# A two-layer decoder trunk in fp32: conditioning summed beside the heads' projections, branch sums on VectorE, value matmuls of 512 columns

## The chip, the core and the metric

The kernel runs on one core of a Trainium2 chip. The metric is the device time of one execution in microseconds (us). A core has TensorE (PE) for matmuls, VectorE (DVE), ScalarE (ACT) and GpSimd (POOL) for elementwise work, and SyncE (SP), on whose queue this kernel issues its DMAs. Each engine runs its instructions in the order in which the program lists them, and semaphores make it wait for the others.

## The reference, cut to what matters

Two layers over a sequence of 512 with 1024 channels, all in float32. Each layer conditions its input with scales and shifts that are computed from a vector `c`, runs three branches (retention, a gated linear recurrence called HGRN2, a causal convolution of 31 taps with its own layer norm), merges them with sigmoid gates, projects, and normalizes; then a feed-forward part with a norm of its own.

```python
cond = jax.nn.silu(c)
for l in range(DEPTH):
    mod = cond @ w_ada[l] + b_ada[l]
    sh1, sc1, g1, sh2, sc2, g2 = [m[:, None, :] for m in jnp.split(mod, 6, axis=-1)]
    h = x * (1.0 + sc1) + sh1
    y = _token_mixer(h, ...)
    x = _layer_norm(ALPHA * x + g1 * y, ln1_g[l], ln1_b[l])
    h = x * (1.0 + sc2) + sh2
    y = _conv_ffn(h, ...)
    x = _layer_norm(ALPHA * x + g2 * y, ln2_g[l], ln2_b[l])

# in _token_mixer: p = h @ w_in, split into rq, rk, rv, rg, gq, gf, gi, gg, ca, cb, gates
u = _causal_dwconv(ca * jax.nn.sigmoid(cb), conv_w, conv_b)      # 31 taps, 512 channels
u_c = jax.nn.silu(_layer_norm(u, conv_ln_g, conv_ln_b))
gates = jax.nn.sigmoid(gates.reshape(bsz, s, N_BRANCH, D_MODEL))
y = gates[:, :, 0] * (u_a @ w_branch[0])
y = y + gates[:, :, 1] * (u_b @ w_branch[1])
y = y + gates[:, :, 2] * (u_c @ w_branch[2])
return y @ w_out
```

## The kernel before, in words

Channels lie on the 128 partitions, the 512 positions along the free axis. Each float32 product is made of three matmuls (`mm3`, L249 to L251): every operand is kept as a high part and a low part, and high·high, high·low and low·high are added up in one PSUM tile. Weights come in chunks of 512 KB (128 x 1024 float32). `prefetch` issues the DMA (L215, tile `wr`), copies the high part on ScalarE (L216, `wh`) and subtracts the low part on VectorE (L217, `wl`); `chunk` keeps two chunks ahead of the matmuls. A projection of 128 channels is 24 matmuls of 512 columns on one chunk (`proj`, tile `pm`).

The conditioning `cond @ w_ada` does not run on PE: each of its 96 columns is a chunk of 512 KB that is loaded (L191, tile `ar`) and multiplied and summed on VectorE (L195, then L196). Its tile has the tag `raw`, with four buffers, and these are the buffers of the weight chunks too.

A layer goes through these stages: the projections for the convolution; ten steps of heads (`MIX`: for HGRN2 and for retention, a projection of the values for all four heads by `proj_tok`, and three projections for each head, with the head's own small matmuls run beside the next head's projections); the three branches in the order HGRN2, retention, convolution (`ORDER = (1, 0, 2)`, by index 1, 0, 2), where each step makes two gate projections and two branch products (L249 to L251 with a `b` tile as input), multiplies them (L782) and adds them to the sum (L786 on GpSimd, tile `ys`); the output projection with the first norm; and the feed-forward part.

Work that PE does not need soon runs as generators. `tick`, called within each projection, adds to a credit; while the credit is positive the generators in `heads` and in the list `fill` are stepped, and what each step yields is taken off. `fill` holds, in this order, the tables for the rotation, the convolution's taps (`conv_taps`, two times two tiles, L383), its norm (`conv_norm`: totals on GpSimd L396 to L398, `exact2` L236 and L237, a column sum on PE L243 and L245, subtraction L408, square L410, totals and column sum again, `rstd` L308 to L311, product L421, SiLU L422, `split` L229 and L231), and the remaining conditioning (`rest`). Before the third branch's first product a loop sees to it that the norm is issued:

```python
while b == 2 and len(u_c) < 4:
    step(fill, fill[0])
```

The generators fix what is issued, and with which priority; a scheduler then sets each engine's order, from its own estimate of when each instruction can run.

Of the kernel before, what the change touches and what calls it, by code (L numbers as in the profile page):

```python
# [20 lines left out]
P = 128  # L21
KT = D // P
# [6 lines left out]
EPS = 1e-5  # L29
NB = 47  # L30
NHL = 4
LA = 2
NRAW = 4
TK = 1.7
AUX = 99
TG = 1.1
# [17 lines left out]
def w_plan(l):  # L54
    conv = [SEG[s] + 128 * i for i in range(4) for s in ("cb", "ca")]
    if l == 0:
        plan = [("octo", k, conv) for k in range(8)]
    else:
        plan = [("quad", k, conv[:4]) for k in range(4)]
        plan += [("in", c) for c in conv[4:]]  # L60

    def tok(seg):
        return [("tok", c, SEG[seg] + 256 * g) for g in range(2) for c in range(2)]

    for what, i in MIX:
        if i < 0:
            plan += tok("gi" if what == "g" else "rv")
        else:
            names = ("gf", "gq", "gg") if what == "g" else ("rq", "rk", "rg")
            plan += [("in", SEG[n] + 128 * i) for n in names]  # L70
    for b in ORDER:
        for jp in range(4):
            c = SEG["gates"] + D * b + 256 * jp
            plan += [("in", c), ("in", c + 128), ("br", b, jp)]
    plan += [("out", j) for j in range(8)]
    plan += [("upq", k, [0, DFF, 128, DFF + 128]) for k in range(4)]
    for j in range(2, FT):
        plan += [("up", j), ("up", FT + j)]
    plan += [("down", c) for c in range(FT)]
    return plan  # L80
# [9 lines left out]
def trunk(ctx, tc, xT, cT, pos, ada, bada, wts, cols, lbl, rope_c, decay, hmask, outT):  # L90
# [97 lines left out]

    def ada_col(l, i):
        raw = wp.tile([P, 1024], F32, tag="raw", name=nm("ar"), bufs=NRAW)  # L190
        nc.sync.dma_start(raw, ada[l, i])  # L191
        o = ADA[i]
        dst = modt[l][:, o:o + 1]
        yield 0.0
        stt(raw, raw, 1.0, cond, ALU.mult, ALU.mult, accum_out=dst)  # L195
        ts(dst, dst, bad[:, 48 * l + o:48 * l + o + 1], 1.0 if o // 8 in (1, 4) else 0.0, ALU.add, ALU.add)  # L196
        yield 1.3

# [91 lines left out]
    def proj_tok(hs):  # L290
        for g in range(2):
            w = [chunk("tok", LA - 1), chunk("tok", LA - 1)]
            for tp in range(2):
                q = pm()
                for t2 in range(2):
                    tk = 2 * tp + t2
                    dst = q[:, 256 * t2:256 * (t2 + 1)]
                    for kt in range(KT):
                        mm3(dst, sl2(hs[kt], 128 * tk), sl2(w[kt // 4], 256 * (kt % 4), 256),
                            kt == 0, kt == KT - 1)  # L300
                    tick(1.5)
                yield g, tp, q

# [70 lines left out]

    def conv_taps(l, i0, us, out, aux):

# [4 lines left out]
        for d in range(1, CK):  # L381
            for i, a in enumerate(acc):
                stt(a[:, d:S], us[i][:, 0:S - d], col(l, "cw", 4 * (CK - 1 - d) + i0 + i), a[:, d:S],  # L383
                    ALU.mult, ALU.add)
            yield 1.2
            if d % AUX == 0 and aux:
                yield from aux.pop(0)

    def rest(aux):
        while aux:  # L390
            yield from aux.pop(0)

# [252 lines left out]
    def affine(l, gname, bname, lm, sc, sh):  # L645
        for j in range(8):
            G, B = gbt[:, j:j + 1], gbt[:, 8 + j:9 + j]
            tt(G, col(l, gname, j), mod(lm, sc, j), ALU.mult)
            stt(B, col(l, bname, j), mod(lm, sc, j), mod(lm, sh, j), ALU.mult, ALU.add)
        o = CO[gname]  # L650
        ts(gbt[:, 16:24], colt[l][:, o:o + 8], ALPHA, None, ALU.mult)
        o = CO[bname]
        ts(gbt[:, 24:32], colt[l][:, o:o + 8], ALPHA, None, ALU.mult)

    def norm_to_h(nrm, hs, a, b):
# [37 lines left out]
    for j in range(8):  # L693
        cs = [ada_col(0, 2 * j), ada_col(0, 2 * j + 1)]
        for g in cs:
            next(g)
        nc.sync.dma_start(X[j], xT[j])
        for g in cs:
            next(g)
        prefetch()  # L700
# [7 lines left out]
    for l in range(L):  # L708
# [4 lines left out]
        CS = [big(), big()]  # L713
        aux = [ada_col(l, i) for i in range(16, 40)]
        if l == 0:
            tables()
        fill.append(rope_tables(CS))
        for i in (0, 2):
            us = []
            for t in range(2):  # L720
                if not qs:
                    qs = [proj(chunk("in"), hs), proj(chunk("in"), hs)]
                us.append(conv_gate(qs.pop(0), qs.pop(0)))
            fill.append(conv_taps(l, i, us, acc, aux))
        fill.append(conv_norm(l, acc, u_c))
        fill.append(rest(aux))

        vg, vr = [big() for _ in range(4)], [big() for _ in range(4)]
        for what, h in MIX:
            if what == "g" and h < 0:  # L730
                for g, tp, q in proj_tok(hs):
                    for t2 in range(2):
                        act(vg[2 * tp + t2][:, 256 * g:256 * (g + 1)], q[:, 256 * t2:256 * (t2 + 1)], AF.Copy)
            elif h < 0:
                for g, tp, q in proj_tok(hs):
                    qv = q.rearrange("p (t h d) -> p t h d", h=2, d=128)
                    sm = bp.tile([P, 4], F32, tag="sm", name=nm("sm"), bufs=2)
                    nc.vector.tensor_reduce(sm, q.rearrange("p (a d) -> p a d", d=128),
                                            mybir.AxisListType.X, ALU.add)
                    for t2 in range(2):  # L740
                        stt(vr[2 * tp + t2][:, 256 * g:256 * (g + 1)].rearrange("p (h d) -> p h d", d=128),
                            sm[:, 2 * t2:2 * t2 + 2].unsqueeze(2).broadcast_to([P, 2, 128]), -1.0 / 128,
                            qv[:, t2], ALU.mult, ALU.add)
            elif what == "g":
                qf = proj(chunk("in"), hs)
                qq = proj(chunk("in"), hs)
                qg = proj(chunk("in"), hs)
                drain(heads, 2)
                heads.append(hgrn_head(l, h, *hgrn_gates(l, h, qq, qf, qg), vg, u_b))
            else:  # L750
                q = rope(proj(chunk("in"), hs), *CS)
                k = rope(proj(chunk("in"), hs), *CS)
                qg = proj(chunk("in"), hs)
                sg = big()
                act(sg, qg, AF.Silu)
                drain(heads, 2)
                heads.append(ret_head(l, h, q, k, sg, vr, u_a))

        ys = [None] * 8
        for bi, b in enumerate(ORDER):  # L760
            us = (u_a, u_b, u_c)[b]
            for jp in range(4):
# [13 lines left out]
                for t in range(2):  # L776
# [14 lines left out]
        affine(l, "ln1g", "ln1b", l, 4, 3)  # L791
        nrm = Norm(l, 2)
# [26 lines left out]

        fill.extend(ada_col(l, i) for i in range(40, 48))  # L820
        gs = []
# [19 lines left out]
        if l == 0:  # L841
            fill.extend(ada_col(1, i) for i in range(16))
        nrm = Norm(l, 5)
        hs = []
        held = []
        for j in range(8):
            parts = HALVES if j == 7 else ((0, S),)
            if l == 0 and j == 7:
                drain(fill)
                affine(l, "ln2g", "ln2b", 1, 1, 0)  # L850
            for a, b in parts:
# [38 lines left out]
def _chunks(l, w_in, w_branch, w_out, w_up, w_down):  # L890
    out = np.empty((NW, 128, 1024), np.float32)
    down = w_down.reshape(FT, 128, 8, 128).transpose(2, 0, 1, 3).reshape(FT, 8, 128, 128)
    for i, p in enumerate(W_PLAN[l]):
# [10 lines left out]
        elif p[0] == "tok":  # L904
            out[i] = _ktile(w_in, 4 * p[1], 4, p[2], 256)
        elif p[0] == "br":
# [77 lines left out]
```

## Time and profile before

| | us |
|---|---|
| median of 3 runs | 1848.71 (1846.3 to 1849.69) |
| the profiled execution | 1850.63 |
| its span (first to last instruction) | 1848.5 |
| PE busy | 1805.8 (98%) |
| VectorE busy | 1292.6 (70%) |
| ScalarE busy | 748.4 (40%) |
| GpSimd busy | 225.8 (12%) |
| weight chunks | 299 DMAs of 512 KB, median 3.5 from issue to landing |
| conditioning chunks | 96 DMAs of 512 KB, median 4.3 |

An instruction's duration reaches from its start to its end. On PE matmuls overlap, so the durations of neighbours add up to more than the time they take; the distance between starts is what one of them costs. The same holds, by a smaller part, on VectorE. In the rows below, "idle before" in brackets is the time in which the engine waited before the instruction, with what ended it. PEclk is the granted TensorE clock as a share of 2.4 GHz.

### The profile page before, as it was taken

The page shows a single profiled execution, that of the slowest core. Times are in us where ns is not written, and L with a number is a line of the kernel's source. Part 1 is how long each engine was busy: PE and PEld are TensorE (multiplying, and loading weights), DVE is VectorE, ACT ScalarE, POOL GpSimd, SP SyncE. Part 2 cuts the span into 40 slices and gives each one's busy share as a digit, 9 for nine tenths or more (in the row PEclk, how much of TensorE's full clock was granted, in tenths as well). Part 3 has the DMA queues.
Part 4 walks back from the last instruction along what each step waited for, and adds up shares of the span by engine and source line. Part 5 has one row for each costly group of instructions (what it writes and reads, how often), then busy time and mean ns, then how long its engine had stood idle before and what let it go on. Part 6 is the DMA issues. An engine that isn't in the chain of part 4 may idle for free.

```text
span 1848.5 us, 23499 instructions
## 1 busy us (share of the span) xinstructions
PE 1805.8 (98%) x9156; PEld 1520.1 (82%) x9156; DVE 1292.6 (70%) x2026; ACT 748.4 (40%) x1034; POOL 225.8 (12%) x193
## 2 busy tenths in 40 slices
PE   7999999999999999999999999999999999999997
PEld 5888877888788888888889987778788988888886
DVE  6995565977869756667499565993775896666354
ACT  2434344333337444422263344453523464444222
POOL 3111231042100000000000221320322000000002
PEclk9999999999989999999999999999999999999998
DMA  8512222226614422255222121222474243222221
GB/s 301 197 69 80 75 75 80 91 104 212 230 70 142 144 102 92 102 182 184 93 87 103 69 75 69 80 74 99 161 241 148 92 146 128 103 92 102 92 80 46
DMA packets 63614, 217.81 MB, mean 118 GB/s; under 512 B 7440, under 2 KB 9872, under 8 KB 63504
## 3 DMA queue, kind: packets, MB, share of 16 engines
q1 hardware_dynamic: 63504, 216.32, 34.0%
q8 instruction: 72, 1.18, 0.3%
q14 instruction: 38, 0.31, 0.0%
HBM read 214.19 MB, written 2.10 MB: 117 GB/s over the span
## 4 chain that ended last, share of the span: by engine, by line
PE 81%; DVE 10%; DMA 3%; issue 2%; POOL 2%; ACT 2%; POOLq 0%; SPq 0%; DVEq 0%; ACTq 0%
PE pm L249 24%; PE pm L251 24%; PE pm L250 24%; DMA ar<-ada 3%; DVE wl L217 2%; PE ps L477 2%; POOL b L786 1%; DVE ar L195 1%; DVE b L383 1%; DVE x L642 1%; PE po L552 1%; PE ps L544 1%; DVE b L782 1%; PE ps L250 1%; PE ps L251 0%
## 5 line engine op out<-in xcount | busy, mean ns | idle before, releaser
L249 PE MATMUL pm<-h,wh 128*128 128x512 f32 (+1 forms) x1568 | 612.7, 391 | 13.7 <-ACT wh L216 12.1
L251 PE MATMUL pm<-h,wl 128*128 128x512 f32 (+1 forms) x1568 | 602.6, 384 | 0.1
L250 PE MATMUL pm<-h,wh 128*128 128x512 f32 (+1 forms) x1568 | 601.6, 384 | 0.0
L217 DVE TENSOR_TENSOR wl<-wr,wh 128x1024 fp32r<-128x1024 f32 (+1 forms) x301 | 376.4, 1253 | 250.5 <-ACT wh L216 249.4
L216 ACT ACTIVATE wh<-wr 128x1024 fp32r<-128x1024 f32 (+1 forms) x301 | 317.1, 1055 | 489.3 <-PE pm L250 387.2
L249 PEld LDWEIGHTS pm<-h,wh 128*128 128x128 f32 x1568 | 295.5, 188 | 72.9 <-ACT wh L216 12.1
L251 PEld LDWEIGHTS pm<-h,wl 128*128 128x128 f32 x1568 | 295.0, 188 | 61.1 <-DVE wl L217 3.1
L250 PEld LDWEIGHTS pm<-h,wh 128*128 128x128 f32 x1568 | 295.4, 188 | 58.7 <-issue 1.9
L249 PE MATMUL pm<-b,wh 128*128 128x512 f32 (+1 forms) x764 | 280.6, 367 | 5.6 <-ACT b L229 4.2
L250 PE MATMUL pm<-b,wh 128*128 128x512 f32 (+1 forms) x764 | 279.6, 366 | 0.3 <-DVE b L231 0.2
L251 PE MATMUL pm<-b,wl 128*128 128x512 f32 (+1 forms) x764 | 279.0, 365 | 0.0
L383 DVE SCALAR_TENSOR_TENSOR b<-b,cols,b 128x511 f32<-128x511 f32 (+14 forms) x240 | 171.6, 769 | 0.0
L249 PEld LDWEIGHTS pm<-b,wh 128*128 128x128 f32 x764 | 144.8, 190 | 30.3 <-ACT b L229 5.4
L250 PEld LDWEIGHTS pm<-b,wh 128*128 128x128 f32 x764 | 144.9, 190 | 24.5 <-DVE b L231 1.5
L251 PEld LDWEIGHTS pm<-b,wl 128*128 128x128 f32 x764 | 145.0, 190 | 22.8
L195 DVE SCALAR_TENSOR_TENSOR ar<-ar,cond 128x1024 f32<-128x1024 f32 x96 | 123.8, 1296 | 57.1 <-DMA ar<-ada 56.9
L229 ACT ACTIVATE b<-b 128x512 fp32r<-128x512 f32 x88 | 55.5, 630 | 232.8 <-DVE b L832 109.2
L231 DVE TENSOR_TENSOR b<-b,b 128x512 fp32r<-128x512 f32 x88 | 61.1, 694 | 53.8 <-ACT b L229 53.6
L490 POOL TENSOR_TENSOR b<-b,b 128x256 f32<-128x256 f32 x64 | 56.4, 881 | 324.1 <-PE ps L477 217.3
L786 POOL TENSOR_TENSOR b<-b,b 128x512 f32<-128x512 f32 x32 | 57.2, 1786 | 234.9 <-DVE b L782 222.5
L249 PE MATMUL pm<-wh,h 128*128 128x256 f32 x256 | 73.6, 288 | 0.0
L250 PE MATMUL pm<-wl,h 128*128 128x256 f32 x256 | 72.3, 283 | 0.6 <-DVE wl L217 0.6
(205 smaller groups left out, 1904.1 us busy)
## 6 DMA issues: line engine op xcount, KB each, us to landing
wr<-wts SPq DMA_DIRECT2D x299, 512.0 KB, 3.5
ar<-ada SPq DMA_DIRECT2D x96, 512.0 KB, 4.3
x<-xT SPq DMA_DIRECT2D x8, 256.0 KB, 5.9
b<-decay SPq DMA_DIRECT2D x8, 256.0 KB, 3.7
outT<-b SPq DMA_DIRECT2D x16, 128.0 KB, 1.8
b<-hmask SPq DMA_DIRECT2D x3, 256.0 KB, 5.9
cond<-cT SPq DMA_DIRECT2D x1, 512.0 KB, 4.5
wr<-wts SPq DMA_DIRECT2D x2, 256.0 KB, 7.3
```

Source lines behind the costliest of these rows:

```text
L195: stt(raw, raw, 1.0, cond, ALU.mult, ALU.mult, accum_out=dst)
L216: act(hi[:, s], raw[:, s], AF.Copy)
L217: tt(lo[:, s], raw[:, s], hi.bitcast(F32)[:, s], ALU.subtract)
L229: act(hi, src, AF.Copy)
L231: tt(lo, src, hi.bitcast(F32), ALU.subtract)
L249: mm(dst, a[0], b[0], start=first, stop=False)
L250: mm(dst, a[0], b[1], start=False, stop=False)
L251: last[0] = mm(dst, a[1], b[0], start=False, stop=end)
L383: stt(a[:, d:S], us[i][:, 0:S - d], col(l, "cw", 4 * (CK - 1 - d) + i0 + i), a[:, d:S], ALU.mult, ALU.add)
L477: mm(z[:, 64 * i:64 * (i + 1)], ke[:, sl], rhs, start=True, stop=True)
L490: ptt(kv[:, :, 0, :], kv[:, :, 0, :], fv[:, :, 1:2].broadcast_to([P, nb, m]), ALU.mult)
L786: ptt(ys[j], ys[j], sg[t], ALU.add)
```

## The change

Four parts. Conditioning chunks get buffers of their own (tag `ada`, three of them), and a generator `ada_cols` issues the next load before it sums a column. The 24 columns of a layer's first norm are stepped once per head projection (`proj_cond`), and what a step yields (1.4) is taken off the credit; columns that are left are appended to `fill`, and the affine terms of the norm follow as a generator. The branch sums move from GpSimd (`ptt`) to VectorE (`tt`). `proj_tok` multiplies with 512 columns of weights at a time, so its chunks are cut as two channel tiles by 512 columns, four are held, and a result tile covers one block of 128 positions and all four heads; the evictions follow suit. `conv_taps` no longer carries conditioning. There is one `B` buffer more, and the program is built with `dynamic_dma_scratch_size=1024`.

```diff
+NADA = 3
-AUX = 99
...
     def tok(seg):
-        return [("tok", c, SEG[seg] + 256 * g) for g in range(2) for c in range(2)]
+        return [("tok", c, SEG[seg]) for c in range(4)]
...
-    def ada_col(l, i):
-        raw = wp.tile([P, 1024], F32, tag="raw", name=nm("ar"), bufs=NRAW)
+    def ada_load(l, i):
+        raw = wp.tile([P, 1024], F32, tag="ada", name=nm("ar"), bufs=NADA)
         nc.sync.dma_start(raw, ada[l, i])
+        return raw
+
+    def ada_sum(l, i, raw):
         o = ADA[i]
         dst = modt[l][:, o:o + 1]
-        yield 0.0
         stt(raw, raw, 1.0, cond, ALU.mult, ALU.mult, accum_out=dst)
         ts(dst, dst, bad[:, 48 * l + o:48 * l + o + 1], 1.0 if o // 8 in (1, 4) else 0.0, ALU.add, ALU.add)
-        yield 1.3
+
+    def ada_cols(l, idx):
+
+        raw = None
+        for i, j in zip(idx, [*idx[1:], None]):
+            if raw is None:
+                raw = ada_load(l, i)
+                yield 0.2
+            nxt = None if j is None else ada_load(l, j)
+            ada_sum(l, i, raw)
+            raw = nxt
+            yield 1.4
...
     def proj_tok(hs):
-        for g in range(2):
-            w = [chunk("tok", LA - 1), chunk("tok", LA - 1)]
-            for tp in range(2):
-                q = pm()
+
+
+        w = []
+        for tp in range(2):
+            qs = [pm(), pm()]
+            for c in range(4):
+                if tp == 0:
+                    w.append(chunk("tok", LA if c < 2 else 3 - c))
                 for t2 in range(2):
-                    tk = 2 * tp + t2
-                    dst = q[:, 256 * t2:256 * (t2 + 1)]
-                    for kt in range(KT):
-                        mm3(dst, sl2(hs[kt], 128 * tk), sl2(w[kt // 4], 256 * (kt % 4), 256),
+                    for k in range(2):
+                        kt = 2 * c + k
+                        mm3(qs[t2], sl2(hs[kt], 128 * (2 * tp + t2)), sl2(w[c], 512 * k, 512),
                             kt == 0, kt == KT - 1)
-                    tick(1.5)
-                yield g, tp, q
+                    if t2:
+                        tick(1.5)
+            for t2 in range(2):
+                yield 2 * tp + t2, qs[t2]
...
-        aux = [ada_col(l, i) for i in range(16, 40)]
+        aux = ada_cols(l, range(16, 40))
...
-            fill.append(conv_taps(l, i, us, acc, aux))
+            fill.append(conv_taps(l, i, us, acc))
         fill.append(conv_norm(l, acc, u_c))
-        fill.append(rest(aux))
+
+        def proj_cond(hs):
+
+            credit[0] -= next(aux, 0.0)
+            return proj(chunk("in"), hs)
...
-                qf = proj(chunk("in"), hs)
-                qq = proj(chunk("in"), hs)
-                qg = proj(chunk("in"), hs)
+                qf, qq, qg = [proj_cond(hs) for _ in range(3)]
...
+        fill.append(aux)
+        fill.append(affine(l, "ln1g", "ln1b", l, 4, 3))
...
-                        ptt(ys[j], ys[j], sg[t], ALU.add)
+                        tt(ys[j], ys[j], sg[t], ALU.add)
...
-        fill.extend(ada_col(l, i) for i in range(40, 48))
+        fill.append(ada_cols(l, range(40, 48)))
...
-            fill.extend(ada_col(1, i) for i in range(16))
+            fill.append(ada_cols(1, range(16)))
```

In the changed file the line numbers are higher: the sum of a column is L197 and L198, a weight's parts are L228 to L230, `mm3` is L262 to L264, the column sum L256 and L258, the taps L401, the norm's subtraction L420, `rstd` L326 to L329, the branch's product L795 and its sum L799.

The first place is PE in layer 0, around the second column sum of the convolution's norm. `pm_3371` and `pm_3389` are the branch products of a step of the second branch, `po_3384` is the column sum; the first column sum (`po_3294`) stands 50 rows above it, and the first matmul on the convolution's result 132 rows below it. Before:

```order
L250 MATMUL pm_3371<-b_2746,wh_3276 128x512
L251 MATMUL pm_3371<-b_2744,wl_3277 128x512
L243 MATMUL po_3384<-b_3347,avg_r 128x512
L245 MATMUL po_3384<-b_3348,avg_r 128x512
L249 MATMUL pm_3389<-b_2072,wh_3276 128x512
L250 MATMUL pm_3389<-b_2074,wh_3276 128x512
```

Now `pm_3387` is the second gate projection of the third branch, `po_3439` and `po_3463` are the two column sums, and `pm_3502` is the first product on the convolution's result (`b_3474`, `b_3476`):

```order
L262 MATMUL pm_3387<-h_265,wh_3307 128x512
L263 MATMUL pm_3387<-h_266,wh_3307 128x512
L264 MATMUL pm_3387<-h_265,wl_3308 128x512
L256 MATMUL po_3439<-b_3435,avg_r 128x512
L258 MATMUL po_3439<-b_3436,avg_r 128x512
L256 MATMUL po_3463<-b_3459,avg_r 128x512
L258 MATMUL po_3463<-b_3460,avg_r 128x512
L262 MATMUL pm_3502<-b_3474,wh_3347 128x512
L263 MATMUL pm_3502<-b_3476,wh_3347 128x512
```

The matmuls between the two column sums, and those between the second one and its reader, have gone from there; in layer 1 the same rows are neighbours too.

The second place is VectorE in layer 0 at the last taps. Before, they end in the second branch (`b_2783` and `b_2784` are the last pair's sums, `pm_3236` a product of the second branch):

```order
L782 TENSOR_TENSOR b_3112<-pm_3137,b_3112 128x512
L217 TENSOR_TENSOR wl_3193<-wr_3191,wh_3192 128x1024
L383 SCALAR_TENSOR_TENSOR b_2784<-b_508,cols_272,b_2784 128x483
L383 SCALAR_TENSOR_TENSOR b_2783<-b_505,cols_272,b_2783 128x482
L383 SCALAR_TENSOR_TENSOR b_2784<-b_508,cols_272,b_2784 128x482
L217 TENSOR_TENSOR wl_3232<-wr_3230,wh_3231 128x1024
L217 TENSOR_TENSOR wl_3277<-wr_3275,wh_3276 128x1024
L782 TENSOR_TENSOR b_3189<-pm_3236,b_3189 128x512
```

Now the product on `pm_3329`, the last matmuls of the second branch, stands before the last 18 taps (`b_3046` and `b_3047`), of which the first four are shown; the others follow without anything between, down to 128x482:

```order
L230 TENSOR_TENSOR wl_3348<-wr_3346,wh_3347 128x1024
L795 TENSOR_TENSOR b_3304<-pm_3329,b_3304 128x512
L401 SCALAR_TENSOR_TENSOR b_3046<-b_505,cols_272,b_3046 128x490
L799 TENSOR_TENSOR b_2832<-b_2832,b_3304 128x512
L401 SCALAR_TENSOR_TENSOR b_3047<-b_508,cols_272,b_3047 128x490
L230 TENSOR_TENSOR wl_3383<-wr_3381,wh_3382 128x1024
L401 SCALAR_TENSOR_TENSOR b_3046<-b_505,cols_272,b_3046 128x489
L401 SCALAR_TENSOR_TENSOR b_3047<-b_508,cols_272,b_3047 128x489
```

The taps' end has moved from the second branch to after its end. In layer 1 the last tap stands just before VectorE's product on the last matmuls of the second branch.

The third place is SP's queue in layer 0's heads. Before, the loads of weights stand there alone:

```order
L215 DMA wr_1266<-wts 128x1024
L215 DMA wr_1272<-wts 128x1024
L215 DMA wr_1456<-wts 128x1024
L215 DMA wr_1462<-wts 128x1024
L215 DMA wr_1506<-wts 128x1024
```

Now conditioning loads (`ar`) stand between them, up to eight in a row:

```order
L228 DMA wr_1324<-wts 128x1024
L191 DMA ar_1807<-ada 128x1024
L191 DMA ar_1886<-ada 128x1024
L191 DMA ar_1957<-ada 128x1024
L191 DMA ar_2012<-ada 128x1024
L191 DMA ar_2083<-ada 128x1024
L191 DMA ar_2146<-ada 128x1024
L191 DMA ar_2219<-ada 128x1024
L191 DMA ar_2282<-ada 128x1024
L228 DMA wr_1378<-wts 128x1024
```

All of the later columns' loads have moved into layer 0, those of the feed-forward part and of layer 1 too; before, the first of them after the start stands in the third branch.

## Rows read from the trace of the kernel before

**Rows 1.** The page: span, PE's busy time, the chain that ended last.

```profile
span 1848.5 us, 23499 instructions
...
PE 1805.8 (98%) x9156; PEld 1520.1 (82%) x9156; DVE 1292.6 (70%) x2026; ACT 748.4 (40%) x1034; POOL 225.8 (12%) x193
...
PE 81%; DVE 10%; DMA 3%; issue 2%; POOL 2%; ACT 2%; POOLq 0%; SPq 0%; DVEq 0%; ACTq 0%
```

**Rows 2.** Timeline of PE, 480 to 520: start, duration, operation, idle before.

```profile
499.43 0.39 PE L251 MATMUL pm<-b,wl 128*128 128x512 f32 x1
...
511.70 0.80 PE L249 MATMUL pm<-b,wh 128*128 128x512 f32 x1 [2.29 <-ACT b L229]
...
518.09 0.40 PE L251 MATMUL pm<-b,wl 128*128 128x512 f32 x1
```

**Rows 3.** Windows: length, busy of PE, PEld, DVE, ACT, POOL; PEclk, DMA share, GB/s.

```profile
60.00:400.00 340.00, 338.57 (x1855) 286.35 (x1856) 252.38 (x381) 137.76 (x195) 62.05 (x58) 1.00 0.25 86
512.00:518.00 6.00, 6.00 (x14) 4.41 (x14) 2.26 (x3) 1.06 (x1) 0.00 (x0) 0.50 0.30 100
1110.00:1250.00 140.00, 135.79 (x653) 106.16 (x653) 120.36 (x175) 64.53 (x92) 35.06 (x28) 1.00 0.21 72
```

**Rows 4.** The chain of waits, 400 to 520: start, length, what.

```profile
486.81 4.63 DMA ar<-ada
...
497.89 3.33 DMA wr<-wts
```

**Rows 5.** The page's groups: busy and mean ns of one, idle before.

```profile
L249 PE MATMUL pm<-h,wh 128*128 128x512 f32 (+1 forms) x1568 | 612.7, 391 | 13.7 <-ACT wh L216 12.1
...
L195 DVE SCALAR_TENSOR_TENSOR ar<-ar,cond 128x1024 f32<-128x1024 f32 x96 | 123.8, 1296 | 57.1 <-DMA ar<-ada 56.9
...
L249 PE MATMUL pm<-wh,h 128*128 128x256 f32 x256 | 73.6, 288 | 0.0
```

**Rows 6.** Timeline of PE, value projection of layer 0, 64 to 70.

```profile
63.89 0.28 PE L249 MATMUL pm<-wh,h 128*128 128x256 f32 x1
...
69.89 0.28 PE L250 MATMUL pm<-wl,h 128*128 128x256 f32 x1
```

**Rows 7.** Timeline of PE, projections, 340 to 345.

```profile
339.97 0.39 PE L249 MATMUL pm<-h,wh 128*128 128x512 f32 x1
...
344.95 0.39 PE L250 MATMUL pm<-h,wh 128*128 128x512 f32 x1
```

**Rows 8.** Timeline of VectorE: weight part, taps, the norm's subtraction.

```profile
339.28 1.23 DVE L217 TENSOR_TENSOR wl<-wr,wh 128x1024 fp32r<-128x1024 f32 x1
340.42 4.03 DVE L383 SCALAR_TENSOR_TENSOR b<-b,cols,b 128x507 f32<-128x507 f32 x6
...
403.19 2.48 DVE L408 SCALAR_TENSOR_TENSOR b<-po,b 128x512 f32<-128x512 f32 x4
```

**Rows 9.** Timeline of GpSimd, the norm's totals and low part, layer 0.

```profile
391.06 2.21 POOL L397 TENSOR_TENSOR b<-b,b 128x512 f32<-128x512 f32 x1 [1.23 <-DVE b L383]
393.34 1.29 POOL L398 TENSOR_TENSOR b<-b,b 128x512 f32<-128x512 f32 x1
396.49 1.33 POOL L237 TENSOR_TENSOR b<-b,b 128x512 fp32r<-128x512 f32 x1 [1.85 <-ACT b L236]
...
407.91 2.37 POOL L397 TENSOR_TENSOR b<-b,b 128x512 f32<-128x512 f32 x1 [1.39 <-ACT b L410]
```

**Rows 10.** Timeline of ScalarE, the norm's root, SiLU and copies, layer 0.

```profile
415.05 0.69 ACT L308 ACTIVATE b<-po,eps_c 128x512 f32<-128x512 f32 x1
...
425.69 1.52 ACT L422 ACTIVATE b<-b,cols 128x512 f32<-128x512 f32 x2 [6.19 <-DVE b L421]
427.11 0.62 ACT L229 ACTIVATE b<-b 128x512 fp32r<-128x512 f32 x1
427.64 0.80 ACT L422 ACTIVATE b<-b,cols 128x512 f32<-128x512 f32 x1
```

**Rows 11.** Timeline of PE, the second column sum, layer 0.

```profile
413.90 0.40 PE L243 MATMUL po<-b,avg_r 128*128 128x512 f32 x1
```

More of the change, by code (lines that the diff above doesn't have):

```diff
@@ L29 @@
 EPS = 1e-5
-NB = 47
+NB = 48
 NHL = 4
@@ L373, in conv_gate, with conv_taps @@
         return sg
-    def conv_taps(l, i0, us, out, aux):
+    def conv_taps(l, i0, us, out):
         acc = [big(), big()]
@@ L385, in conv_taps @@
             yield 1.2
[L386 to L391, printed above, removed]
     def conv_norm(l, acc, out):
@@ L649, in affine @@
             stt(B, col(l, bname, j), mod(lm, sc, j), mod(lm, sh, j), ALU.mult, ALU.add)
+            yield 0.4
         o = CO[gname]
@@ L653, in affine @@
         ts(gbt[:, 24:32], colt[l][:, o:o + 8], ALPHA, None, ALU.mult)
+        yield 0.4
     def norm_to_h(nrm, hs, a, b):
@@ L693, in trunk @@
     for j in range(8):
-        cs = [ada_col(0, 2 * j), ada_col(0, 2 * j + 1)]
-        for g in cs:
-            next(g)
+        cs = [ada_load(0, 2 * j), ada_load(0, 2 * j + 1)]
         nc.sync.dma_start(X[j], xT[j])
-        for g in cs:
-            next(g)
+        for t, raw in enumerate(cs):
+            ada_sum(0, 2 * j + t, raw)
         prefetch()
@@ L730, in trunk @@
             if what == "g" and h < 0:
-                for g, tp, q in proj_tok(hs):
-                    for t2 in range(2):
-                        act(vg[2 * tp + t2][:, 256 * g:256 * (g + 1)], q[:, 256 * t2:256 * (t2 + 1)], AF.Copy)
+                for tk, q in proj_tok(hs):
+                    act(vg[tk], q, AF.Copy)
             elif h < 0:
-                for g, tp, q in proj_tok(hs):
-                    qv = q.rearrange("p (t h d) -> p t h d", h=2, d=128)
+                for tk, q in proj_tok(hs):
+                    qv = q.rearrange("p (h d) -> p h d", d=128)
                     sm = bp.tile([P, 4], F32, tag="sm", name=nm("sm"), bufs=2)
[L738 to L743, printed above, removed]
+                    nc.vector.tensor_reduce(sm, qv, mybir.AxisListType.X, ALU.add)
+                    stt(vr[tk].rearrange("p (h d) -> p h d", d=128),
+                        sm.unsqueeze(2).broadcast_to([P, 4, 128]), -1.0 / 128, qv, ALU.mult, ALU.add)
             elif what == "g":
-                qf = proj(chunk("in"), hs)
-                qq = proj(chunk("in"), hs)
-                qg = proj(chunk("in"), hs)
+                qf, qq, qg = [proj_cond(hs) for _ in range(3)]
                 drain(heads, 2)
@@ L750, in trunk @@
             else:
-                q = rope(proj(chunk("in"), hs), *CS)
-                k = rope(proj(chunk("in"), hs), *CS)
-                qg = proj(chunk("in"), hs)
+                q = rope(proj_cond(hs), *CS)
+                k = rope(proj_cond(hs), *CS)
+                qg = proj_cond(hs)
                 sg = big()
@@ L790, in trunk @@
         drain(fill)
-        affine(l, "ln1g", "ln1b", l, 4, 3)
         nrm = Norm(l, 2)
@@ L849, in trunk @@
                 drain(fill)
-                affine(l, "ln2g", "ln2b", 1, 1, 0)
+                for _ in affine(l, "ln2g", "ln2b", 1, 1, 0):
+                    pass
             for a, b in parts:
@@ L904, in _chunks @@
         elif p[0] == "tok":
-            out[i] = _ktile(w_in, 4 * p[1], 4, p[2], 256)
+            out[i] = _ktile(w_in, 2 * p[1], 2, p[2], 512)
         elif p[0] == "br":
@@ L974 @@
     }
-    nc = _bacc.Bacc("TRN2", target_bir_lowering=False, num_devices=1)
+    nc = _bacc.Bacc("TRN2", target_bir_lowering=False, num_devices=1, dynamic_dma_scratch_size=1024)
     args = [nc.dram_tensor(n, v.shape, mybir.dt.from_np(v.dtype), kind="ExternalInput").ap()
```

## The prediction

> **What bounds the kernel now.** I read the page first. PE is busy for 1805.8 of 1848.5 us and the chain that ended last is 81% PE [rows 1], so only what shortens PE's own stream, or stops it, can move the time. The second view is PE's timeline in the few stretches where the stream breaks. The largest break lies at the end of layer 0's branch stage: from the matmul at 499.43 to the one at 518.09 there are 36 steps, which at the usual 0.227 us (below) would take 8.17 us and took 18.66, so 10.5 us are lost there: waits, the last of 2.29 us, and then a stretch at half clock [rows 2, 3]. The third view is the chain of waits just before: DMAs of the conditioning (`ar<-ada`) and one late weight load (`wr<-wts`) are its longest pieces [rows 4]; both kinds take the same four buffers there, so a weight load stands behind conditioning that waits for VectorE. Everything else is covered by PE.
>
> **Value matmuls (wide).** Each layer's two value projections issue 2 x 192 = 384 matmuls of 256 columns; 192 of 512 columns replace them, so 384 pairs go over both layers. By the mean of one in the page's groups (288 against 391 ns [rows 5]) a pair would give 2 x 288 - 391 = 185 ns, 71 us in all. But matmuls overlap, and the step is what counts: 63.89 to 69.89 is 50 steps of 0.120 us at 256 columns, 339.97 to 344.95 is 22 steps of 0.226 us at 512 [rows 6, 7]. A pair gives 0.240 - 0.227 = 0.013 us: 384 x 0.013 = 5.0 us. I take 5.
>
> The Trainium skill's page "TensorE: Matmul & The Clock Gate" (section Back-to-back issue gap) has a step of columns / 2.4 plus 2.5 ns: 109.2 and 215.8 ns, so 2.6 ns for a pair and about 1 us in all. The rows show a larger fixed part, 0.120 and 0.226; the forecast goes by the rows.
>
> **Conditioning: own buffers and an earlier place.** The 24 columns of each layer's first norm leave the branch stage, and weight loads no longer share their buffers. I count the 10.5 us at 499 to 518 as gone. What it costs: the instruction order now has all of the later sums, 80 beyond the 16 at the start, spread over layer 0's heads and first branches. VectorE was busy 252.4 of 340 us there [rows 3]. One sum is 1.30 us plus two short ones, about 1.4 [rows 5], so 80 of them are 112 and the sum of durations is 364, 24 us more than PE's 340. But durations overlap as well: a weight's low part of 1.23 holds the next instruction back for only 1.14, from 339.28 to 340.42 [rows 8]. With these 7% off, the sum is 338, about PE's 340. So the cost lies between 0 and 24; I take 5, near the lower end, since the steps are what the queue pays. Layer 1's heads lost 140.0 - 135.8 = 4.2 us of PE time in a stretch with VectorE busy 120.4 of 140 [rows 3]; sums and taps move out of it, and I give back 3. Net 2.
>
> **Branch sums on VectorE.** 32 adds leave GpSimd for VectorE, where a 128x512 operation takes 0.62 us (four in 2.48 [rows 8]): 32 x 0.62 = 20 us of VectorE over both layers, in a stage where PE works 48 x 0.227 = 10.9 us on the two projections alone for each pair of adds. PE hides them: 0. Were VectorE full there, all 20 would show.
>
> **The convolution's norm comes onto PE's path.** This is the large term. Each head projection now also charges the background credit with 1.4 for its column, so the taps, which live on that credit, run late, and `while b == 2 and len(u_c) < 4` issues all of the norm at one place. Before, PE has 48 matmuls between the two column sums and 132 rows from the second to the first matmul that reads the result. In the changed order the two column sums and that matmul are neighbours, in both layers: PE, which takes matmuls in order, must wait out the whole chain.
>
> The Trainium skill's page "TensorE: Matmul & The Clock Gate" (section The mechanism) has matmuls start and end strictly in program order. By it nothing further down can fill the wait, and the stalls below stand in full; were later matmuls to overtake, rival 1 would hold. No row here shows one that overtakes.
>
> Layer 0. Let T be the end of the last matmul of the second branch. VectorE waits for it (the product with the gate), and behind that stand the branch add (0.62 each), 18 taps (4.03 / 6 = 0.67 each) and one weight part (1.14): 2 x 0.62 + 18 x 0.67 + 1.14 = 14.4 us [rows 8].
> Taps to first sum: two GpSimd adds 2 x 1.29, copy 0.62, low part 1.33, four hand-overs of some 0.08 (393.34 after 391.06 + 2.21), two matmuls to their result 0.23 + 0.40: 5.5 [rows 9 to 11].
> First sum to second: four subtractions 2.48, the last square like a copy 0.62, then 2 x 1.29, 0.62, 1.33, five hand-overs, 0.63: 8.7 [rows 8 to 11]. Before, from 403.19 to 413.90 it took 10.7 beside other work.
> Second sum to PE: root 0.69, three operations and the first product 4 x 0.6, then four SiLU and four copies alternating on ScalarE (0.71 and 0.53 a step) 5.0, hand-overs 0.3, last low part and matmuls 0.9: 9.3, less the 12 matmuls that run anyway, 2.7: 6.6 [rows 8, 10].
> Together 35.2. PE covers the first two projections of the third branch, 48 x 0.227 = 10.9, and the four column sums' own 0.9: a stall of 23.4. GpSimd is beside VectorE's two weight parts for an add or two, +1: 24.
>
> Layer 1. There the last taps stand ahead of VectorE's wait for the end of the second branch, so their 5.5 hide under the 10.9. What stays is 0.6 + 8.7 + 6.6 less 0.9, 15.0; one weight part stands in the middle of the chain on VectorE: 16.
>
> Bounds of both: 38 if every step runs as in quiet and nothing interrupts it; with GpSimd at 2.21 to 2.37 for its adds and low parts, as beside VectorE before, where 1.29 is the quiet value [rows 9], and VectorE and ScalarE as interrupted as before, about 10 to 14 more, 52. Below nothing is excluded, since no other matmul stands between. I take 40.
>
> **Clock.** After the waits at 501 to 511 PE ran 512 to 518 at a granted clock of 0.50, 1.2 GHz: 14 steps in 6.39 us instead of 3.18 [rows 2, 3]. Both new stalls are longer, so I add 3 us after each: 6 (between 0 and 10).
>
> **Sum.** Against the profiled execution of 1850.6 us (span 1848.5 and 2.1 around it; 1.9 above the median of the three runs): 1850.6 + 24 + 16 + 6 + 2 - 5 - 10.5 = 1883. Taken to the median: 1881.
>
> **The rivals.**
> 1. The chain stays hidden: the norm's instructions find work on PE, or taps run early enough. Then 1850.6 - 5 - 10.5, with 0 to 5 for the heads: 1835 to 1840. For it: the same chain cost PE next to nothing before. Against it: the order has no PE instruction there. Chance 0.09.
> 2. VectorE becomes the bound of layer 0: weights' low parts come late behind 80 sums, and weight loads stand on SP's queue behind up to eight conditioning loads, each of which waits for a buffer that a sum frees. It decides once the queue needs more than PE's 340 us; at the durations' sum it costs 24 rather than 5: 1881 + 19 = 1900, up to 1910 with the layer's later sums. For it: the sum of durations, and 86% busy already lost PE time [rows 3]. Against it: the steps. Chance 0.15.
> 3. The wide matmuls give what the group means say: 71 instead of 5, 1881 - 66 = 1815. Against it: PE's steps at 64 us. Chance 0.02.
> 4. The chain is shorter than worked out, only one layer stalls (the 16 of layer 1 gone, its clock stretch too): 1881 - 19 = 1862; in half of such cases the gains bring it near 1850. Chance 0.10.
> My forecast, both stalls of about this size, has 0.64.
>
> **How the numbers follow.** The forecast's own range is 1870 to 1897: stalls 38 to 52, clock 0 to 10. The 8-in-10 range takes in most of rivals 2 and 4: 1853 to 1908; outside lie rivals 1 and 3 with 0.11 and small tails. A measurement of this kernel tells 0.2%, 3.7 us, from no change. Faster: rivals 1 and 3 and a little of 4, 0.12; within: 0.03, out of 4; slower: 0.85.
>
> **What the profile of the changed kernel would show.** On PE, waits for POOL or ACT at the first column sum (layer 0 only, some 9 us), at the second (7 to 8, both layers), and for ACT before the first matmul on the conv result (5 and more, both layers); a granted clock of 0.5 after each; no break where 499 to 518 was; 512-column steps of 0.227 in the value projections; no `ar` DMA in the chain of the branch stage. I would be wrong if the column sums were passed without a wait, or if PE waited many times by a microsecond for `wl` in layer 0's heads: that would be rival 2.

## The result, and the profile after

The changed kernel takes 1881.78 us (median of 4 runs, 1878.9 to 1882.23), the kernel before 1849.2 beside it: a ratio of 1.017, interval 1.0158 to 1.0182. It is slower by 32.6 us. The profiled execution took 1878.9 us, 28.3 more than that of before.

The page of the changed kernel: PE's share has fallen from 98% to 96% [rows 1], though its work is shorter, and the chain that ended last has more VectorE in it.

```profile
span 1877.1 us, 22746 instructions
...
PE 1804.0 (96%) x8772; PEld 1499.8 (80%) x8772; DVE 1294.8 (69%) x2050; ACT 748.8 (40%) x1025; POOL 167.9 (9%) x161
...
PE 79%; DVE 14%; issue 3%; ACT 2%; POOL 1%; DMA 1%; SPq 0%; POOLq 0%; DVEq 0%; ACTq 0%
```

PE's timeline at the third branch of layer 0 (start, duration, operation, idle before with its releaser). L256 and L258 are a column sum, the L262 at 475.41 is the first product on the convolution's result:

```profile
449.49 0.39 PE L264 MATMUL pm<-h,wl 128*128 128x512 f32 x1
458.77 0.79 PE L256 MATMUL po<-b,avg_r 128*128 128x512 f32 x1 [8.89 <-ACT b L249]
460.12 0.79 PE L258 MATMUL po<-b,avg_r 128*128 128x512 f32 x1 [0.55 <-POOL b L250]
467.51 0.79 PE L256 MATMUL po<-b,avg_r 128*128 128x512 f32 x1 [6.61 <-ACT b L249]
468.86 0.80 PE L258 MATMUL po<-b,avg_r 128*128 128x512 f32 x1 [0.55 <-POOL b L250]
475.41 0.80 PE L262 MATMUL pm<-b,wh 128*128 128x512 f32 x1 [5.75 <-ACT b L242]
476.13 0.80 PE L263 MATMUL pm<-b,wh 128*128 128x512 f32 x1
...
479.71 0.43 PE L262 MATMUL pm<-b,wh 128*128 128x512 f32 x1
```

From 449.49 to 475.41 PE made five steps, 1.1 us of work, in 25.9 us: 24.8 us are lost. Layer 1 has the same without the first wait; the same view there:

```profile
1383.12 0.79 PE L256 MATMUL po<-b,avg_r 128*128 128x512 f32 x1 [7.59 <-ACT b L249]
1384.46 0.79 PE L258 MATMUL po<-b,avg_r 128*128 128x512 f32 x1 [0.55 <-POOL b L250]
1391.01 0.79 PE L262 MATMUL pm<-b,wh 128*128 128x512 f32 x1 [5.75 <-ACT b L242]
```

By the distances between starts that makes 15.2 us. VectorE's timeline shows why the wait in layer 0 begins as it does: the product on the second branch's last matmuls at 439.46, then the last 18 taps (the first two among other work, 16 in the row of 443.08), two weight parts, the norm's subtraction, and the first step of its root:

```profile
439.46 0.69 DVE L795 TENSOR_TENSOR b<-pm,b 128x512 f32<-128x512 f32 x1
...
443.08 10.25 DVE L401 SCALAR_TENSOR_TENSOR b<-b,cols,b 128x489 f32<-128x489 f32 x16
453.25 2.35 DVE L230 TENSOR_TENSOR wl<-wr,wh 128x1024 fp32r<-128x1024 f32 x2
460.94 2.48 DVE L420 SCALAR_TENSOR_TENSOR b<-po,b 128x512 f32<-128x512 f32 x4 [5.34 <-PE po L258]
470.41 0.69 DVE L327 SCALAR_TENSOR_TENSOR b<-po,b 128x512 f32<-128x512 f32 x1 [6.98 <-ACT b L326]
```

GpSimd's timeline there holds the step that was much longer than in the working, an add of the first total beside the two weight parts; the next row is an add in quiet:

```profile
453.47 3.25 POOL L409 TENSOR_TENSOR b<-b,b 128x512 f32<-128x512 f32 x1 [121.84 <-DVE b L401]
456.80 1.26 POOL L410 TENSOR_TENSOR b<-b,b 128x512 f32<-128x512 f32 x1
```

Three windows of the changed kernel, layer 0's heads, the end of the first stall, and layer 1's heads (columns as in [rows 3]):

```profile
60.00:345.00 285.00, 276.47 (x1388) 223.12 (x1387) 279.29 (x507) 119.27 (x169) 56.56 (x52) 1.00 0.60 203
468.00:480.00 12.00, 5.70 (x13) 3.47 (x13) 7.25 (x11) 7.74 (x11) 0.80 (x1) 0.51 0.00 0
1138.00:1260.00 122.00, 121.12 (x577) 96.43 (x576) 69.73 (x105) 59.04 (x83) 25.78 (x24) 1.00 0.22 76
```

And the kernel before in the first of them:

```profile
60.00:345.00 285.00, 283.57 (x1613) 240.76 (x1614) 203.34 (x318) 123.02 (x176) 50.36 (x51) 1.00 0.24 82
```

VectorE went from 203 to 279 of 285 us: 66 of the 96 conditioning sums start in this stretch now, none before. PE's distances above the usual step went from 10 to 21 us between 60 and 340. The longest of the new waits end with a conditioning sum (total us, times, longest; `mod` is the sum's result):

```profile
PE po L256 <- DVE mod L198: 3.3, 2, 1.7
```

In layer 1 it is the reverse: 15 before, 10 now. The value projections step as the other ones do now (against 0.120 for half the columns in [rows 6]): 24 steps in 5.44 us, 0.227 each.

```profile
64.00 0.39 PE L264 MATMUL pm<-wh,h 128*128 128x512 f32 x1
...
69.44 0.39 PE L264 MATMUL pm<-wh,h 128*128 128x512 f32 x1
```

The account of the 28.3 us of the profiled executions, by distances between starts: stalls at the norm +24.8 and +15.2, their half-clock stretches +4.2, layer 0's heads +11, layer 1's heads -5; the break at 499 to 518 [rows 2] gone with a short wait ahead of it, -11.3; shorter value matmuls -5; two waits of layer 1's branch stage -3; the start and the rest about -2. They add up to 29.

### The profile page after: what moved, and what is told of

The parts are those of the page before. It is cut to its first block, busy times and chain, and to the rows that moved or that the text cites. A ratio compares the mean times of both kernels' runs of the same rounds, so it can differ in the third digit from the quotient of the medians.

```text
span 1877.1 us, 22746 instructions
## 1 busy us (share of the span) xinstructions
PE 1804.0 (96%) x8772; PEld 1499.8 (80%) x8772; DVE 1294.8 (69%) x2050; ACT 748.8 (40%) x1025; POOL 167.9 (9%) x161
## 4 chain that ended last, share of the span: by engine, by line
PE 79%; DVE 14%; issue 3%; ACT 2%; POOL 1%; DMA 1%; SPq 0%; POOLq 0%; DVEq 0%; ACTq 0%
PE pm L262 24%; PE pm L264 24%; PE pm L263 24%; DVE b L401 2%; DVE ar L197 2%; DVE wl L230 2%; PE ps L489 1%; DMA ar<-ada 1%; DVE b L501 1%; PE ps L556 1%; DVE x L654 1%; PE ps L263 1%; PE po L564 1%; ACT h L678 1%; PE ps L264 1%
## 5 line engine op out<-in xcount | busy, mean ns | idle before, releaser
L262 PE MATMUL pm<-h,wh 128*128 128x512 f32 (+1 forms) x1568 | 612.6, 391 | 12.6 <-ACT wh L229 10.9
L264 PE MATMUL pm<-h,wl 128*128 128x512 f32 (+1 forms) x1568 | 603.2, 385 | 0.1
L230 DVE TENSOR_TENSOR wl<-wr,wh 128x1024 fp32r<-128x1024 f32 (+1 forms) x301 | 371.0, 1236 | 330.3 <-ACT wh L229 329.4
L262 PEld LDWEIGHTS pm<-h,wh 128*128 128x128 f32 x1568 | 295.4, 188 | 71.7 <-ACT wh L229 10.9
L264 PEld LDWEIGHTS pm<-h,wl 128*128 128x128 f32 x1568 | 295.0, 188 | 60.7 <-DVE wl L230 2.5
L262 PE MATMUL pm<-b,wh 128*128 128x512 f32 (+1 forms) x764 | 280.7, 367 | 11.5 <-ACT b L242 11.5
L264 PE MATMUL pm<-b,wl 128*128 128x512 f32 (+1 forms) x764 | 278.9, 365 | 0.0
L262 PEld LDWEIGHTS pm<-b,wh 128*128 128x128 f32 x764 | 145.1, 190 | 35.7 <-ACT b L242 12.5
L264 PEld LDWEIGHTS pm<-b,wl 128*128 128x128 f32 x764 | 144.9, 190 | 22.4
L401 DVE SCALAR_TENSOR_TENSOR b<-b,cols,b 128x511 f32<-128x511 f32 (+14 forms) x240 | 161.8, 735 | 0.0
L197 DVE SCALAR_TENSOR_TENSOR ar<-ar,cond 128x1024 f32<-128x1024 f32 x96 | 123.9, 1305 | 13.7 <-DMA ar<-ada 13.5
L839 DVE SCALAR_TENSOR_TENSOR b<-pm,cols,b 128x510 f32<-128x510 f32 x84 | 62.8, 749 | 2.7
L837 ACT ACTIVATE b<-pm,cols 128x512 f32<-128x512 f32 x84 | 63.7, 760 | 0.0
L843 ACT ACTIVATE b<-b 128x512 f32<-128x512 f32 x44 | 27.8, 633 | 89.3 <-DVE b L839 89.3
```

The lines of the kernel that those rows point to most:

```text
L230: tt(lo[:, s], raw[:, s], hi.bitcast(F32)[:, s], ALU.subtract)
L262: mm(dst, a[0], b[0], start=first, stop=False)
L264: last[0] = mm(dst, a[1], b[0], start=False, stop=end)
L837: act(a, q, AF.Identity, bias=col(l, "fb", i), scale=col(l, "fw", 88 + i))
L839: stt(a[:, 2:S], q[:, 0:S - 2], col(l, "fw", i), a[:, 2:S], ALU.mult, ALU.add)
```

## The experiments

Most ask what one or two parts are worth. Each was timed beside the kernel before, on the same chip; ratios are to that kernel.

**No charge on the credit.** The changed kernel with

```diff
-            credit[0] -= next(aux, 0.0)
+            next(aux, 0.0)
```

> The changed kernel without the charge on the credit: each head projection still steps one column, but takes nothing off. In its order the two column sums of the norm stand 50 rows apart again in both layers; the sums stay in layer 0's heads. Theory (the charge delays the taps, and the norm's chain then stands on PE): the stalls of 24.8 and 15.2 us and their half-clock stretches of about 4 go, and taps that return to layer 0's heads cost up to 10: 1838 to 1848 us, against 1881.8. Rival (VectorE's queue, full of early sums, is what PE waits for): the sums are as early as before, so it stays above 1870.

Measured: 1850.18 us, ratio 1.0002 (0.9993 to 1.0011). 31.6 us came back, so the rival, a full VectorE queue alone, falls. But the time lies above the range I gave: PE still loses 24 us in layer 0's heads (10 before the change, 21 with the charge), and the taps, which are back among the sums, end so late that the first column sum still waits:

```profile
426.55 0.50 PE L256 MATMUL po<-b,avg_r 128*128 128x512 f32 x1 [3.20 <-ACT b L249]
428.10 0.80 PE L258 MATMUL po<-b,avg_r 128*128 128x512 f32 x1 [1.05 <-POOL b L250]
```

**No columns in the head projections.** The line above removed altogether.

> The changed kernel, but no column is stepped in the head projections: all 24 stand behind the norm in the background list. With buffers of their own the scheduler still starts the sums early, about 120 VectorE rows later than in the changed kernel. Theory: no stall at the column sums, fewer early sums in layer 0's first heads: 1834 to 1844 us, the same as or up to 4 below the kernel without the charge. Rival (it matters that the sums run beside the projections): slower than that kernel by more than 3.

Measured: 1850.79 us, ratio 1.0007 (0.9999 to 1.0016), the same as the last one. It makes no difference whether the heads' code asks for the sums: the scheduler pulls them there anyway. Between 60 and 345 us 63 of them start here, and 64 with the last edit. Both my ranges left out what the pull costs.

**Buffers of their own, in the kernel before.**

```diff
-        raw = wp.tile([P, 1024], F32, tag="raw", name=nm("ar"), bufs=NRAW)
+        raw = wp.tile([P, 1024], F32, tag="ada", name=nm("ar"), bufs=NADA)
```

(with `NADA = 3` and the smaller DMA scratch, as in the change)

> The kernel before with one edit: the conditioning loads get three buffers of their own (and the DMA scratch is cut to make room). Theory (weight loads behind conditioning in shared buffers make the break of 10.5 us at 499 to 518): that break goes; the scheduler moves the sums into layer 0's heads, which costs 0 to 11: 1838 to 1849 us. Rival (the break comes from the branch sums on GpSimd): the break stays and the time is 1849 to 1860.

Measured: 1862.51 us, ratio 1.0067 (1.0053 to 1.008): slower, outside both ranges. The break at 499 to 518 is gone, as the theory has it, but PE loses 27 us in layer 0's heads instead of 10, and the first column sum waits, 9 us with what follows. Its window of layer 0's heads has VectorE full:

```profile
60.00:345.00 285.00, 272.00 (x1540) 227.19 (x1539) 272.16 (x501) 115.35 (x169) 55.02 (x51) 0.99 0.58 198
```

So buffers of their own are enough for the pull; that the turn in the shared ones had kept a sum in its place is the reading that fits. The smaller DMA scratch came with them, but it is not what costs: a kernel below that has both as well, and sums kept in place, takes 1838.31 us.

**Value matmuls of 512 columns, in the kernel before.** The edits of `tok`, `proj_tok`, its evictions and the packing of the chunks, as in the change.

> The kernel before with one edit: value projections of 512 columns. By the steps on PE (0.120 and 0.227 us) 384 pairs give 0.013 each: 5.0 us less, 1844.2 us. By columns / 2.4 plus 2.5 ns: 1.0 less, 1848.2. By the group means: 71 less, 1778.

Measured: 1843.88 us, ratio 0.9969 (0.9956 to 0.9981), 3.5 to 8 us less. The steps' 5.0 lie inside; 1.0 and 71 do not.

**The sums kept in place, the charge kept.** The changed kernel with

```diff
+                part[0] = tt(lo[:, s], raw[:, s], hi.bitcast(F32)[:, s], ALU.subtract)
...
-            ada_sum(l, i, raw)
+            with tc.issue_after(part[0].ins):
+                ada_sum(l, i, raw)
```

so that a sum stands on VectorE behind the weight part issued last before it.

> The changed kernel with one edit: each column's sum is queued on VectorE behind the weight part that was issued last, so the scheduler can't pull the sums of later stages into layer 0's heads. The charge stays, and the two column sums of the norm are still neighbours in both layers. Theory (two separate costs: the charge puts the norm on PE, some 40 us and its clock; own buffers let the scheduler pull 80 sums forward, some 10 to 14 us): only the second goes, 1865 to 1874 us. Rival (one cost, a full VectorE queue, behind both): 1850 or less.

Measured: 1873.76 us, ratio 1.0128 (1.0112 to 1.0145), in the theory's range. PE's loss in layer 0's heads is 12 us, against 10 before the change and 21 in the changed kernel, and the norm still stands on PE with nearly the same waits:

```profile
451.60 0.79 PE L258 MATMUL po<-b,avg_r 128*128 128x512 f32 x1 [9.66 <-ACT b L251]
...
460.35 0.80 PE L258 MATMUL po<-b,avg_r 128*128 128x512 f32 x1 [6.61 <-ACT b L251]
...
468.25 0.79 PE L264 MATMUL pm<-b,wh 128*128 128x512 f32 x1 [5.76 <-ACT b L244]
```

**Kept in place, no charge.** Both edits together.

> The same pacing, and no charge on the credit: one column per head projection, the norm's column sums 50 rows apart again. Theory: stalls at the column sums gone, early sums gone, no break at the end of the branch stage, wide value matmuls kept: 1830 to 1840 us. Rival (own buffers cost the 12 us by something else than the pull forward, such as the DMAs' number in flight): 1846 to 1852, as without pacing.

Measured: 1832.98 us, ratio 0.9911 (0.9896 to 0.9926). Against the last one 40.8 us: that is the charge by itself. (With the pull in place it was 31.6: without the charge the taps stand among the early sums there, and PE waits for both.) Against the kernel without pacing 17.2: that is the pull. The window of layer 0's heads:

```profile
60.00:345.00 285.00, 282.81 (x1428) 231.05 (x1427) 237.60 (x400) 122.64 (x173) 55.88 (x52) 1.00 0.38 129
```

Here 23 sums do start beside the heads' projections, and PE is busy for 282.8 of 285 us, against 283.6 before the change.

**Kept in place, after the norm.** Pacing, and no columns in the head projections.

> The same pacing, no column in the head projections: the 24 sums run after the norm, in the branch stage, as before the change, but from buffers of their own, with wide value matmuls and branch sums on VectorE. Theory: 1849 less 5 (matmuls) less 10 (break at 499 to 518): 1830 to 1837 us, within 3 of the kernel with one column per projection. Rival (the break comes from VectorE's or the branch sums' work there, not from shared buffers): 1842 to 1848.

Measured: 1830.02 us, ratio 0.9893 (0.9879 to 0.9908), 51.8 below the changed kernel. The two places of the columns, heads or branch stage, are 3 us apart in favour of the old one, but the intervals overlap, so a difference is not shown.

**The norm on VectorE, in the changed kernel.** `ptt` becomes `tt` in the totals of `conv_norm`, and `exact2` becomes `split`.

> The changed kernel with one edit: the norm's totals and low parts run on VectorE instead of GpSimd. Theory (PE waits for the chain's own length): the second total and low part are shorter by about 1.9 us in each layer (1.29 and 1.33 become about 0.6 each), the first of layer 0 is about even since two weight parts stand between, so 3 to 6 us less than the changed kernel, 1876 to 1879. Rival (PE waits for something else, a weight or a buffer, at the column sums): no change, 1881 to 1883.

Measured: 1876.9 us, ratio 1.0146 (1.0131 to 1.0162), 4.9 below the changed kernel; the two intervals just touch, so the waits say more than the time. The waits at the second column sum fell from 6.61 to 5.35 in layer 0, and from 7.59 to 6.30 in layer 1; the waits for the result stayed at 5.76. The first two rows are of layer 0, the last two of layer 1:

```profile
465.47 0.80 PE L256 MATMUL po<-b,avg_r 128*128 128x512 f32 x1 [5.35 <-ACT b L242]
472.75 0.79 PE L262 MATMUL pm<-b,wh 128*128 128x512 f32 x1 [5.76 <-ACT b L242]
...
1379.45 0.79 PE L256 MATMUL po<-b,avg_r 128*128 128x512 f32 x1 [6.30 <-ACT b L242]
1386.73 0.79 PE L262 MATMUL pm<-b,wh 128*128 128x512 f32 x1 [5.75 <-ACT b L242]
```

So PE waits for the length of this chain, and a link made shorter shows in the wait right behind it.

**Branch sums on VectorE, in the kernel before.** The one line `ptt` to `tt`.

> The kernel before with one edit: the branch sums on VectorE. Theory (the break at 499 to 518 comes from the shared buffers, the adds lie beside PE): the break stays, 1846 to 1851 us against 1849.7. Rival (the slow GpSimd adds at the end of the branch stage are what PE waits for): the break goes, 1838 to 1842.

Measured: 1834.59 us, ratio 0.9917 (0.9903 to 0.993), below both ranges. This was the miss that taught most: the break is gone altogether, with the shared buffers still in place, and 15.6 us with it. The window where it was, and VectorE's two costly operations from 400 to 500 (busy, mean ns), in this kernel:

```profile
480.00:520.00 40.00, 40.00 (x178) 33.11 (x177) 29.29 (x47) 14.51 (x19) 0.00 (x0) 1.00 0.49 166
```

```profile
L195 DVE SCALAR_TENSOR_TENSOR ar<-ar,cond 128x1024 f32<-128x1024 f32 x24 | 29.1, 1221 | 12.4 <-DMA ar<-ada 12.3
L217 DVE TENSOR_TENSOR wl<-wr,wh 128x1024 fp32r<-128x1024 f32 x19 | 23.1, 1218 | 0.3 <-ACT wh L216 0.2
```

and the same two groups in the kernel before:

```profile
L195 DVE SCALAR_TENSOR_TENSOR ar<-ar,cond 128x1024 f32<-128x1024 f32 x23 | 31.3, 1366 | 15.7 <-DMA ar<-ada 15.7
L217 DVE TENSOR_TENSOR wl<-wr,wh 128x1024 fp32r<-128x1024 f32 x16 | 22.8, 1425 | 0.1
```

Sums and weight parts had been 0.15 to 0.2 us longer on average, and in that stage a buffer comes free when such an operation ends. The adds are what lengthens them: in the kernel before, the 17 sums of this stretch that no GpSimd instruction overlaps took 1.22 us, the slowest 1.23, and those that one overlaps up to 2.32. Two such meetings in the kernel before, on VectorE and then on GpSimd: at 400.9 the add starts first and keeps its 1.29 us, and the weight part takes 2.34; at 407.9 the weight part starts first and keeps its 1.22, and the add takes 2.37.

```profile
400.88 2.34 DVE L217 TENSOR_TENSOR wl<-wr,wh 128x1024 fp32r<-128x1024 f32 x1
...
407.90 1.22 DVE L217 TENSOR_TENSOR wl<-wr,wh 128x1024 fp32r<-128x1024 f32 x1
```

```profile
400.85 1.29 POOL L786 TENSOR_TENSOR b<-b,b 128x512 f32<-128x512 f32 x1 [1.49 <-DVE b L782]
...
407.91 2.37 POOL L397 TENSOR_TENSOR b<-b,b 128x512 f32<-128x512 f32 x1 [1.39 <-ACT b L410]
```

The page of this kernel shows the sum of it: with 32 adds more, VectorE's busy time rose from 1292.6 us [rows 1] by 2.5 only, since its other work became shorter.

```profile
PE 1799.7 (98%) x9156; PEld 1518.8 (83%) x9156; DVE 1295.1 (71%) x2058; ACT 749.0 (41%) x1034; POOL 168.1 (9%) x161
```

The adds' own length counts too: on VectorE one takes 0.69 us, and on GpSimd the last two, of 1.26 and 2.11, stand right before PE's last two waits of the break. No run separates the two ways.

**Buffers of their own and sums in place, in the kernel before.** GpSimd still adds.

> The kernel before with buffers of their own for the conditioning loads, and each sum queued on VectorE behind the weight part issued last; branch sums stay on GpSimd, value matmuls at 256 columns. Theory (the shared buffers make the break): 10 us go, 1836 to 1841. Rival (it takes the branch sums on VectorE too): 1842 to 1849.

Measured: 1838.31 us, ratio 0.9938 (0.9925 to 0.9952), 11.8 less: this too removes most of the break. One wait of 1.6 us stays at its end. So the break needs both, the branch sums on GpSimd and buffers in turn; either edit ends nearly all of it.

**The paced kernel with the branch sums back on GpSimd.**

> The fastest kernel so far (own buffers, sums paced and after the norm, wide value matmuls, branch sums on VectorE; 1830.0 us) with the branch sums back on GpSimd. Theory (they are worth nothing once the buffers are apart): 1829 to 1833. Rival: they hold PE at the end of the branch stage, 1836 or more.

Measured: 1835.72 us, ratio 0.9921 (0.9908 to 0.9935), 5.7 above the paced kernel with sums on VectorE: between my theory's range and the rival's. PE waits at the end of the branch stage, and its granted clock falls to 0.66 over 503 to 508; here the add itself stands on PE's path. The last add on GpSimd (second fence) took 2.11 us and stands right before:

```profile
502.51 0.49 PE L264 MATMUL pm<-b,wh 128*128 128x512 f32 x1 [2.51 <-ACT b L244]
503.23 0.50 PE L265 MATMUL pm<-b,wh 128*128 128x512 f32 x1 [0.23 <-DVE b L246]
```

```profile
499.69 2.11 POOL L800 TENSOR_TENSOR b<-b,b 128x512 f32<-128x512 f32 x1 [2.13 <-DVE b L796]
```

**Two parts alone: wide value matmuls and sums on VectorE, in the kernel before.**

> The kernel before with two edits: value matmuls of 512 columns, and the branch sums on VectorE. Nothing is done to the conditioning. Theory (these two parts hold all the gain; buffers of its own and another place for the conditioning give nothing once GpSimd is out of VectorE's way): 1834.6 less 5 to 6, 1828 to 1830.5 us, no slower than the kernel with paced sums in buffers of their own (1830.0). Rival (own buffers still give something): 1832 or more.

Measured: 1832.15 us, ratio 0.9898 (0.9881 to 0.9914). By its time it falls to the rival, by 0.15 us, but the kernel before ran at 1851.02 beside it and at 1849.69 beside the paced kernel; the ratios, 0.9898 and 0.9893, are the same within their intervals. Whether buffers of their own are worth a microsecond after these two edits stays open.

## Why the prediction was right, and where it was not

The time was 1881.78 against 1881, and the mechanism of the large term was the one named: the charge pushes the taps late, the norm is issued at one place, and PE waits out its chain in both layers. The order alone showed it, and the experiments with and without the charge, 1873.8 and 1833.0, give it 40.8 us. That the times agree within 1 us is luck: the executions of the changed kernel differ by 3.3 us, and the profiled one took 1878.9 where the sum for it was 1883, with errors of both signs in it. The range, too, was not what its terms give: stalls of 38 to 52 and a clock of 0 to 10 make 1873 to 1897, not 1870. Term by term:

- *The chain in layer 0*, forecast 24, measured 24.8. From the product to the last tap's end it was 13.9 us (439.46 to 453.33) against 14.4. From there to the first subtraction 7.6 against 5.5 with 1 added: the add beside the two weight parts took 3.25, not 2.21. From the subtraction at 460.94 to the root's first step on VectorE at 470.41 it was 9.5; the working has 8.7 and 0.8. From there to the first product on the result it was 5.0 (470.41 to 475.41) against 5.8: PE started as soon as the first of the four copies was there, and its first nine matmuls, at half clock, took longer than the copies that were left.
- *Layer 1*, forecast 16, measured 15.2. The chain was taken as it runs in quiet, with 1 added for a weight part, and so it ran: the engines had little else to do, and one GpSimd add beside that weight part took 2.24 instead of 1.26.
- *Clock*, forecast 6, measured 4.2. After the first stall PE came back to full speed at 479.71, nine matmuls after 475.41; the column sums themselves also show the longer duration of half clock, 0.79.
- *Layer 0's heads*, forecast 5 from bounds of 0 and 24, measured 11. That term was too low, and to that extent rival 2 came true: I took the queue as just fitting because its steps add up to PE's time, but a queue that fits on average still makes PE wait wherever sums stand ahead of what a head needs. Pacing gave 17.2 us back in the kernel without the charge, where the taps are in the queue as well.
- *Layer 1's heads*, -3 forecast, -5 measured. *Value matmuls*: -5, and their experiment's interval is 3.5 to 8.
- *The break at 499 to 518*, -10.5 forecast, -11.3 measured, but **the cause was only half right**. I put it down to the shared buffers, which the break does need, and wrote "PE hides them: 0" for the branch sums. The sums on VectorE alone are worth 15.6 us. The prediction read the chain of waits [rows 4] for the conditioning DMAs that stood in it, and not for what made each link late. The slow adds were in the rows of GpSimd [rows 9], counted only for the norm, and the branch sums themselves stand in that same chain, six times among its longest pieces, three of them here:

```profile
454.59 2.33 POOL b L786
...
505.49 1.27 POOL b L786
...
508.88 2.12 POOL b L786
```

In the sum the miss did not show, because the changed kernel has both edits, and each ends the break.

The Trainium skill's page "SBUF — State Buffer" (section Who interferes with whom) has a VectorE instruction with two SBUF inputs contend with a GpSimd instruction that reads SBUF. These traces agree: 1366 against 1221 ns for a sum and 1425 against 1218 for a weight part with and without GpSimd's adds, and 3.25 against 1.26 us for an add with and without VectorE beside it.

Two small waits of layer 1 (1309 and 1385) that went were not in the forecast, and neither were the start and the rest: together some 5 us, which balanced most of the 6 that the heads lost beyond the forecast. With the branch sums alone on VectorE the waits there, 2.3 us by the trace from 1290 to 1400, fall to 0.2 as well.

## What to carry to other kernels

When background work is paid from one credit, a new item on the bill delays everything behind it: look in the order for what has become neighbour to what on the bound engine, and price the chain between by its quiet durations. A shared buffer can also be a brake: giving work its own buffers may let a scheduler pull it forward until another queue is full, so pace it explicitly. And ask of every link in a chain of waits why it took as long as it did; a neighbour engine may be the reason, and the cheaper edit.

## What was not expected of the hardware

GpSimd's adds cost VectorE time as well: with the 32 adds moved to VectorE, some 20 us of work, its busy time rose by 2.5 us, and the kernel is 15.6 us faster. How much of that comes from VectorE's shorter operations, and how much from shorter adds at the end of the stage, no run separates. And one GpSimd add of 128x512, 1.26 us in quiet, took 3.25 us beside two weight parts on VectorE, while VectorE's two took 2.35, no longer than in quiet: there it was GpSimd that lost.
